# One decoder block on one core: the order of TensorE's instructions for the attention of tiles 4 to 7 is written out by hand

## The chip, the core and the metric

The kernel runs on one core of a Trainium2 chip. The time is the device time of one launch in microseconds (us); the median of three launches before the change is 1340.05 us (1338.88 to 1342.16). The engines go by their profile names: PE is TensorE (PEld its weight loads), DVE is VectorE, ACT is ScalarE, POOL is GpSimd, and SP is the queue that issues the DMAs.

## The reference, cut to what matters

The input x has 1024 tokens of 1024 columns, in float32. Cut to the parts that this case touches:

```
h = rmsnorm(x);  u_pool, q, kv, gates, B, C, X = split(h @ w_in)
y_nsa = gate0 * attend(q, k_cmp, v_cmp)            # 63 compressed keys
      + gate1 * attend(q, k of the 8 best blocks of 64)
      + gate2 * attend(q, k of the last 512 tokens)
x = x + concat(pool_mixer, y_nsa, short_conv) @ w_out
a, g = split(rmsnorm(x) @ ffn_up)                  # 2 x 2816 columns
x = x + (silu(causal_dwconv3(a)) * g) @ ffn_down
```

There are 8 heads of 64 in 2 groups g; a group shares its keys and values. The 8 best blocks come from the compressed scores.

## The kernel before, in words

**Tiles and products.** The 1024 tokens are 8 tiles of 128. Nearly every float32 product is done as three TensorE products, high times high, high times low part and low times high, where the high part is a rounded copy (ACT, line 88) and the low part the rest (DVE or POOL, line 89).

**One attention unit** is (i, g, br): tile i, group g and branch br, where br = 1 is the window (5 key tiles for i >= 4) and br = 0 the selected blocks (i + 1 key tiles). `span` gives the number ns. `scores` makes, for each of 4 heads, an S tile (two products per half, lines 570 and 571), adds the mask and takes the maximum (DVE, line 578), exponentiates into `pb` (ACT, line 581) and scales it (POOL, line 586). From tile 4 on there is one S tile (two PSUM banks), so a head's S waits until line 581 of the head before has read it. `values` takes, for each key tile, four transposes of `pb` into a `tr` bank (`flip`, line 97: the data is TensorE's stationary operand, loaded like weights, and the identity of 128 columns is streamed), splits the bank (`put_pt`, lines 476 and 477), and adds two products to the unit's `acc` bank (lines 607 and 608). `prepare` transposes the queries of a tile, `compressed` makes the compressed scores (lines 508 to 510), its probabilities `pc`, and the penalties `pen` of the blocks left out, which go into rows 96 to 111 of the query operand qB before the scores of br = 0.

**Order of the work.** `attend` walks over the units: it weaves the scores of a unit with the values of the unit before. It is called for tiles 0..3, then (line 805) for tiles 4..7. After this call in the program come: the projection of the pool and convolution parts of all tiles (`project`, lines 832 to 835), the projection of the attention part of tiles 0..3 with `second_norm` into `h2a`, the 22 chunks of `up` for tokens 0..511 (48 products of 512 columns each, lines 853 to 855, into two `fill` banks), 5 pairs of "early down" products into x2 (line 928, 48 products a pair, 6 per bank, added by DVE in line 929), and the projection of tiles 4..7 into x2. The last third of the time is the same for tokens 512..1023.

What an engine runs in which order is decided when the program is built, by a scheduler that goes by a model of the time and prefers what stands earlier in the program. So in the kernel before, attention of tiles 4..7 comes ahead of `up` and "early down" wherever it is ready, and these fill in. Each engine then runs its list in order: an instruction that waits holds up all behind it.

Of the kernel before, what the change touches and what calls it, by code (L numbers as in the profile page):

```python
# [1 line left out]

# [6 lines left out]
F32 = mybir.dt.float32  # L9
F32R = mybir.dt.float32r  # L10
# [18 lines left out]
NEG = -(2.0 ** 100)  # L29
FORCE = 1e6  # L30
QBUF = 1


C_POOL = 0
# [11 lines left out]
def kernel(  # L46
# [430 lines left out]
        dve.tensor_tensor(lo, pt, hi.bitcast(F32), ALU.subtract)  # L477
        return hi, lo

    qAs, pcs, yfs, pos = {}, {}, {}, {}  # L480
    new_s, new_p, m_row = [None], [None], [None]

    def prepare(i):

        qn = at2.tile([P, 512], F32, tag="qn", bufs=1, name=nm("qn"))
        nc.sync.dma_start(qn, qd[i])
        for g in range(2):
            pq = tr()
            for pr in range(2):
                c0 = g * 256 + pr * P  # L490
                flip(pq[:, pr * P : (pr + 1) * P], qn[:, c0 : c0 + P])
# [10 lines left out]
    def compressed(i):  # L502

        sc = tr()
        sc3 = sc.rearrange("p (h n) -> p h n", h=8)
        for h in range(8):
            g, hh = divmod(h, 4)
            pe.matmul(sc3[:, 2 * hh + g, :], qAs[i, g][:, hh, :], kca[g], start=h == 0, stop=False)
            pe.matmul(sc3[:, 2 * hh + g, :], qB[g][i % QBUF][0:66, hh, :], kcb[g][0:66, :], start=False, stop=False)
        pe.matmul(sc3, ident_b, m_cmp[:, i, :].unsqueeze(1).to_broadcast([P, 8, 64]), start=False, stop=True)  # L510
        mx = small(8, "mx8")
        dve.tensor_reduce(mx, sc3, axis=AX.X, op=ALU.max)
# [11 lines left out]
        if i >= 4:  # L524

            pen = at2.tile([P, 2, 16], F32, tag="pen", bufs=1, name=nm("pen"))
            for g in range(2):
                pg = small(64, "pg", bufs=2)
                dve.tensor_reduce(pg, pc[:, g::2, :].rearrange("p h n -> p n h"), axis=AX.X, op=ALU.add)
                p4 = pg.rearrange("p (j k) -> p j k", k=4)  # L530
                imp = small(16, "imp")
                dve.tensor_reduce(imp, p4[:, :, 0:3], axis=AX.X, op=ALU.add)
                dve.scalar_tensor_tensor(imp, p4[:, :, 3], 0.5, imp, ALU.mult, ALU.add)
                dve.scalar_tensor_tensor(imp[:, 1:16], p4[:, 0:15, 3], 0.5, imp[:, 1:16], ALU.mult, ALU.add)
                dve.tensor_tensor(imp, imp, sel_keep[:, i - 4, :], ALU.mult)
# [6 lines left out]
                pp = tr()  # L542
                flip(pp[0:16, 0:P], pen[:, g, :])
                act.activation(qB[g][i % QBUF][96:112, :, :], pp[0:16, 0:P].unsqueeze(1).to_broadcast([16, 4, P]), AF.Copy)


        pc4 = pc.rearrange("p (h g) n -> p g h n", g=2)
        for g in range(2):
# [1 line left out]
                               gat[:, i, 4 * g : 4 * g + 4].unsqueeze(2).to_broadcast([P, 4, 64]), ALU.mult)  # L550
        pt = tr()
        for hh in range(4):
            flip(pt[:, hh * P : (hh + 1) * P], pc[:, 2 * hh : 2 * hh + 2, :].rearrange("p g n -> p (g n)"))
        pcs[i] = put_pt(pt, "c")

    def span(i, br):
        s0 = max(0, i - 4) if br == 1 else 0
        return s0, i + 1 - s0

    def scores(i, g, br, pbs):  # L560
# [5 lines left out]
        for hh in range(4):  # L566
            S = new_s[0]()
            for c in range(nck):
                cols = slice(s0 * P + c * cw, s0 * P + (c + 1) * cw)
                pe.matmul(S[:, c, :cw], qAs[i, g][:, hh, :], kA[br, g][:, cols], start=True, stop=False)  # L570
                pe.matmul(S[:, c, :cw], qB[g][i % QBUF][0:krows, hh, :], kB[br, g][0:krows, cols],  # L571
                          start=False, stop=True)

# [15 lines left out]
            yield  # L589

    def values(i, g, br, pbs):

# [16 lines left out]
            yield  # L609
        if br == 1:  # L610
            return

        if g == 0:
            yfs[i] = at2.tile([P, 4, P], F32, tag="yf", bufs=1, name=nm("yf"))
        yb = at2.tile([P, 4, P], F32, tag="pth", name=nm("yb"))[0:64]
# [4 lines left out]
        if g == 1:  # L620
            if i < NT - 1:
                nc.sync.dma_start(yn[i], yfs[i])

    def weave(a, b, na, nb):

        done_b = 0
        for k in range(na):
            next(a, None)
            while done_b < (k + 1) * nb // na:
                next(b, None)  # L630
                done_b += 1
        for _ in a:
            pass
        for _ in b:
            pass

    def attend(tiles):
        prepare(tiles[0])
        compressed(tiles[0])
        prev = None  # L640
        for u in [(i, g, br) for i in tiles for g in range(2) for br in (1, 0)] + [None]:
            pbs = []
            sg = scores(*u, pbs) if u else iter(())
            vg, nv = iter(()), 0
            if prev:
                vg = values(*prev[0], prev[1])
                nv = span(prev[0][0], prev[0][2])[1] + (prev[0][2] == 1)
            weave(sg, vg, 3, nv)
            if u and u[1:] == (1, 0) and u[0] < tiles[-1]:
                prepare(u[0] + 1)  # L650
                compressed(u[0] + 1)
            prev = (u, pbs)


    f1 = pht.enter_context(tc.tile_pool(name="f1", bufs=7, side="right"))
# [146 lines left out]
    sth = ExitStack()  # L802
    h2p = sth.enter_context(tc.tile_pool(name="h2a", bufs=1, side="right"))
    h2a = [h2p.tile([P, KT, 512], F32R, name=n) for n in ("h2a_hi", "h2a_lo")]
    attend([4, 5, 6, 7])


    def load_wout(rows_, lo_engs):
# [8 lines left out]
            ws.append((wh, wl))  # L817
        return ws

    def project(y, ws, src, lo_eng, xr=None):  # L820

        if xr is None:
            xr = f4()
# [4 lines left out]
        for nh in range(2):  # L828
            wh, wl = ws[nh]
            ps = fill()  # L830
            for k in range(4):
                pe.matmul(ps, yh[:, k, :], wh[:, k, :], start=k == 0, stop=False)
                pe.matmul(ps, yh[:, k, :], wl[:, k, :], start=False, stop=False)
            for k in range(4):
                pe.matmul(ps, yl[:, k, :], wh[:, k, :], start=False, stop=k == 3)
            ns = slice(nh * 512, nh * 512 + 512)
            dve.tensor_tensor(xr[:, ns], ps, xr[:, ns], ALU.add)
        return xr

    def load_y(src):  # L840
# [1 line left out]
        nc.sync.dma_start(y, src)  # L842
        return y

    def up(c, hv, h2, gbank):

        wh, wl = load_w2(up_r, c * P, DFF + c * P, (pool, pool))
        pss = []
        for sub in range(2):
            ps = (gbank if sub else fill)()  # L850
            cols = slice(sub * P, (sub + 1) * P)
            for kt in range(KT):
                pe.matmul(ps, wh[:, kt, cols], h2[0][:, kt, :], start=kt == 0, stop=False)  # L853
                pe.matmul(ps, wh[:, kt, cols], h2[1][:, kt, :], start=False, stop=False)  # L854
                pe.matmul(ps, wl[:, kt, cols], h2[0][:, kt, :], start=False, stop=kt == KT - 1)  # L855
            pss.append(ps)
        a, g = pss
# [44 lines left out]
    for c in range(NCH):  # L902
        v = up(c, 0, h2a, fill)
        nc.sync.dma_start(hid0[c], v)
    sth.close()


    xp = ctx.enter_context(tc.tile_pool(name="x2", bufs=1, side="right"))
    x2 = xp.tile([P, NT, D], F32, name="x2")


    for i in range(4):
        nc.sync.dma_start(x2[:, i, :], xb[i])
    for c0 in range(0, EARLY, 2):
        dhl = [w([P, 2, D]) for w in (whi, wlo)]
        hhl = []
        for k in range(2):
            hhl.append([f2.tile([P, 512], F32R, tag=t, bufs=2, name=nm(t)) for t in ("yh", "yl")])
            hidden_in(c0 + k, *hhl[k], pool)
            down_in(c0 + k, dhl[0][:, k], dhl[1][:, k], pool)  # L920
        for i in range(4):
            tt = slice(i * P, (i + 1) * P)
            for nh in range(2):
                ns = slice(nh * 512, nh * 512 + 512)
                ps = fill()
                for k in range(2):
                    for a, b in ((0, 0), (0, 1), (1, 0)):
                        pe.matmul(ps, hhl[k][a][:, tt], dhl[b][:, k, ns], start=k + a + b == 0, stop=k + a == 2)  # L928
                dve.tensor_tensor(x2[:, i, ns], ps, x2[:, i, ns], ALU.add)


    ws = load_wout((2, 4), (pool, dve))
    for i in range(4, NT):
        project(load_y(yn[i]) if i < NT - 1 else yfs[i], ws, xa[i], dve, x2[:, i, :])


    st3.close()
# [90 lines left out]
```

## Time and profile before

| | |
|---|---|
| median of 3 launches | 1340.05 us |
| profiled execution | 1340.74 us; from its first to its last instruction (the span) 1339.0 us |
| busy share of the span | PE 97%, PEld 81%, DVE 57%, ACT 40%, POOL 38% |
| mean granted TensorE clock | 0.992 of the full 2.4 GHz |
| first `up` product, last "early down" product | 440.45 us, 874.62 us |

All stretches are in us from the span's start. Matmuls overlap in the records, since each row shows a product from its start to its result: what a product costs PE is read from the distance of its start to the next start, and not from its length.

### The profile page before, as it was taken

The numbers are of one execution on the slowest core, as the hardware profiler recorded it, in microseconds if no ns is written. First come the engines' busy times: TensorE is split into PE (matmuls) and PEld (weight loads), VectorE is DVE, ScalarE is ACT, GpSimd is POOL, SyncE is SP. The second block draws the span as 40 slices with busy tenths as digits, with TensorE's granted clock in tenths as the row PEclk, the third lists the DMA queues.
The fourth block names the chain that finished last, engine by engine and source line by source line (L and its number), as shares of the span: only waits on it lengthen the run. The fifth ranks groups of instructions, "written<-read, shape, count | busy, mean of one in ns | idle before, by whom it ended". The sixth has DMA issues, their size and how long they took to land.

```text
span 1339.0 us, 17613 instructions
## 1 busy us (share of the span) xinstructions
PE 1298.8 (97%) x6510; PEld 1081.2 (81%) x6510; DVE 764.2 (57%) x1487; ACT 541.9 (40%) x978; POOL 504.0 (38%) x452
## 2 busy tenths in 40 slices
PE   6999999989988999999999999999999999999998
PEld 5899987678866888888888888777888788888886
DVE  6753456666666545545645667675454545455554
ACT  5442444344465554445444464443232213223330
POOL 3454722341343445344444544533333124222220
PEclk9999999989998999999999999999999999999999
DMA  9021220335432323322222272323242225323321
GB/s 263 14 64 52 81 84 16 97 126 179 154 108 78 110 87 112 94 78 88 79 89 77 93 264 85 95 81 93 63 126 67 76 78 158 93 81 104 99 64 64
DMA packets 143075, 131.02 MB, mean 98 GB/s; under 512 B 10659, under 2 KB 119437, under 8 KB 142989
## 3 DMA queue, kind: packets, MB, share of 16 engines
q1 hardware_dynamic: 142845, 129.80, 31.3%
q8 instruction: 51, 0.84, 0.2%
q14 instruction: 35, 0.29, 0.1%
q10 hardware_dynamic: 144, 0.10, 0.0%
HBM read 107.60 MB, written 22.28 MB: 97 GB/s over the span
## 4 chain that ended last, share of the span: by engine, by line
PE 89%; DVE 4%; DMA 3%; ACT 2%; issue 1%; POOL 0%; SPq 0%; ACTq 0%; DVEq 0%; POOLq 0%
PE dn L972 12%; PE fill L853 9%; PE fill L855 9%; PE fill L854 9%; PE tr L97 4%; PE fill L928 4%; PE upg L853 3%; PE upg L855 3%; PE upg L854 3%; PE S L570 2%; PE fill L211 2%; PE S L571 2%; PE fill L212 2%; PE fill L213 2%; PE acc L608 2%; PE acc L607 2%
## 5 line engine op out<-in xcount | busy, mean ns | idle before, releaser
L89 POOL TENSOR_TENSOR wlo<-wst,whi 128x1024 fp32r<-128x1024 f32 x113 | 273.5, 2434 | 305.4 <-ACT whi L88 305.2
L586 POOL TENSOR_SCALAR pb<-pb,rc,gat 128x640 f32<-128x640 f32 (+7 forms) x128 | 105.4, 825 | 294.1 <-DVE rc L584 276.8
L88 ACT ACTIVATE whi<-wst 128x1024 fp32r<-128x1024 f32 x128 | 131.1, 1055 | 136.0 <-DMA wst<-in_ffn_up_dram 80.7
L853 PE MATMUL fill<-h2a_hi,whi 128*128 128x512 f32 x352 | 141.1, 401 | 0.1
L854 PE MATMUL fill<-h2a_lo,whi 128*128 128x512 f32 x352 | 140.8, 400 | 0.0
L855 PE MATMUL fill<-h2a_hi,wlo 128*128 128x512 f32 x352 | 140.8, 400 | 0.0
L581 ACT ACTIVATE pb<-S,mx 128x640 f32<-128x640 f32 (+7 forms) x128 | 89.3, 699 | 105.8 <-DVE mx L578 96.4
L975 DVE TENSOR_TENSOR x<-dn,x 128x1024 f32<-128x1024 f32 x64 | 78.2, 1221 | 89.0 <-PE dn L972 88.8
L477 DVE TENSOR_TENSOR ptl<-tr,pth 128x512 fp32r<-128x512 f32 x140 | 93.9, 686 | 52.7 <-ACT pth L476 26.1
L476 ACT ACTIVATE pth<-tr 128x512 fp32r<-128x512 f32 x140 | 80.5, 596 | 76.2 <-PE acc L607 38.4
L860 DVE SCALAR_TENSOR_TENSOR f2k<-fill,colw,f2k 128x511 f32<-128x511 f32 x44 | 32.9, 748 | 87.7 <-ACT f2k L859 83.8
L97 PE MATMUL tr<-ident,pb 128*128 128x128 f32 x528 | 82.8, 272 | 0.1
L578 DVE CUSTOM_DVE_ANT_0 S<-S,m_win 128x640 f32<-128x640 f32 (+4 forms) x96 | 57.7, 607 | 41.4 <-PE S L571 40.9
L972 PE MATMUL dn<-dh,hh 128*128 128x512 f32 x256 | 79.1, 391 | 0.5 <-DVE x L975 0.5
L972 PE MATMUL dn<-dh,hl 128*128 128x512 f32 x256 | 79.2, 391 | 0.0
L972 PE MATMUL dn<-dl,hh 128*128 128x512 f32 x256 | 79.0, 390 | 0.0
L570 PE MATMUL S<-blk,qA 128*128 128x320 f32 (+5 forms) x192 | 67.0, 352 | 11.2 <-ACT pb L581 11.2
L97 PEld LDWEIGHTS tr<-ident,pb 128*128 128x128 f32 x528 | 66.0, 140 | 14.5 <-POOL pb L586 0.3
L853 PEld LDWEIGHTS fill<-h2a_hi,whi 128*128 128x128 f32 x352 | 66.3, 188 | 14.0 <-DVE h2a_lo L181 0.4
L855 PEld LDWEIGHTS fill<-h2a_hi,wlo 128*128 128x128 f32 x352 | 66.3, 188 | 13.7
L854 PEld LDWEIGHTS fill<-h2a_lo,whi 128*128 128x128 f32 x352 | 66.3, 188 | 13.5
L853 PE MATMUL upg<-h2b_hi,whi 128*128 128x512 f32 x176 | 69.1, 393 | 1.0 <-ACT whi L88 0.9
(275 smaller groups left out, 3175.8 us busy)
## 6 DMA issues: line engine op xcount, KB each, us to landing
wst<-in_ffn_up_dram SPq DMA_DIRECT2D x88, 512.0 KB, 3.9
wst<-in_ffn_down_dram SPq DMA_DIRECT2D x32, 512.0 KB, 3.6
wst<-in_w_in_dram SPq DMA_DIRECT2D x18, 512.0 KB, 4.1
wst<-in_w_out_dram SPq DMA_DIRECT2D x12, 512.0 KB, 4.3
hid<-f2k SPq DMA_DIRECT2D x22, 256.0 KB, 2.0
f2k<-hid SPq DMA_DIRECT2D x22, 256.0 KB, 2.9
b<-in_x_dram SPq DMA_DIRECT2D x8, 512.0 KB, 7.0
f<-in_x_dram SPq DMA_DIRECT2D x8, 512.0 KB, 4.2
```

The lines of the kernel that those rows point to most:

```text
L88: act.activation(hi, src, AF.Copy)
L89: lo_eng.tensor_tensor(lo, src, hi.bitcast(F32), ALU.subtract)
L97: pe.transpose(out, src, ident[:n, :n])
L476: act.activation(hi, pt, AF.Copy)
L477: dve.tensor_tensor(lo, pt, hi.bitcast(F32), ALU.subtract)
L570: pe.matmul(S[:, c, :cw], qAs[i, g][:, hh, :], kA[br, g][:, cols], start=True, stop=False)
L581: act.activation(pb[:, : ns * P].rearrange("p (c n) -> p c n", c=nck), S, AF.Exp, bias=mx, scale=-1.0, accum_out=sw)
L586: pool.tensor_scalar(pb[:, : ns * P], pb[:, : ns * P], rc, gat[:, i, col : col + 1], ALU.mult, ALU.mult)
L853: pe.matmul(ps, wh[:, kt, cols], h2[0][:, kt, :], start=kt == 0, stop=False)
L854: pe.matmul(ps, wh[:, kt, cols], h2[1][:, kt, :], start=False, stop=False)
L855: pe.matmul(ps, wl[:, kt, cols], h2[0][:, kt, :], start=False, stop=kt == KT - 1)
L972: pe.matmul(ps[:, nh - turn[0], :], h[:, tt], w[:, nh * 512 : nh * 512 + 512], start=k == 0 and h is hh and w is dh, stop=k == n - 1 and h ...
```

## The change

`values` is replaced, for tiles 4..7, by `value_steps`, and `prepare` and `compressed` become generators that stop before each PE instruction with its kind ("t" for a transpose or a 64-column product, "p" for another product) and a place x in its slot. `slots` has one slot per unit: the unit's scores (its heads at 0.02, 0.22, 0.42 and 0.62 of the slot), the values of the unit before (0.08 to 0.95), and, in the slots of the units (i, 1, 0) of tiles 4 to 6, the next tile's queries (0.75), compressed scores (0.92) and, reaching into the next slot, the transposes of pc (1.7) and pen (1.85). The slot of unit (4, 0, 1) (`LEAD` = 1) stands where `attend` stood. The others are merged with `fillers`, that is `up` and then "early down", under a `manual_schedule` for PE alone: PE's instructions of this region run in the order in which they are written, the other engines stay with the scheduler, and so does the place of PE instructions from outside of the region among these. In `merge`, 380 us are shared out among the slots by key tiles; a filler is counted as 0.231 us, a transpose as 0.03 us, any other step as 0.2 us, fillers are laid until the next step's place is reached, and one is put between two "t" steps.

```diff
+STEP = 0.231
+LEAD = 1
+ATT_US = 380.0
...
+    def value_steps(i, g, br, pbs, x0, x1):
+        s0, ns = span(i, br)
+        n = 6 * ns + 4
...
+        for s in range(ns):
+            if br == 1 and s == 1:
+                pos[i, g] = ps2.tile([P, 512], F32, tag="acc", name=nm("acc"))
+                queue[i, g][0:0] = [((i, g), vvc[:, g, :], w, w is pcs[i][0], False) for w in pcs[i]]
+            pt = tr()
+            for hh in range(4):
+                yield "t", x0 + (x1 - x0) * k / n
+                k += 1
+                flip(pt[:, hh * P : (hh + 1) * P], pbs[hh][:, s * P : (s + 1) * P])
+                if hh in (1, 3) and queue[i, g] and not (br == 1 and s == 0):
+                    yield "p", x0 + (x1 - x0) * k / n
+                    k += 1
+                    product()
+            parts = put_pt(pt)
...
+    def merge(slots, us, filler):
...
+                while at < e[0] and fill_one():
+                    at += STEP
+                    short = False
+                at = max(at, e[0])
+                if e[2] == "t" and short and fill_one():
+                    at += STEP
+                if e[2] != "head":
+                    short = e[2] == "t"
+                    at += 0.03 if short else 0.2
...
-    attend([4, 5, 6, 7])
+    second = list(slots([4, 5, 6, 7]))
+    for _, streams in second[:LEAD]:
+        for st in streams:
+            run(st)
...
+        for c0 in range(0, EARLY, 2):
...
+                hhl.append([f2.tile([P, 512], F32R, tag=t, bufs=2, name=nm(t)) if c0 % 4 == 0 else f2k(F32R) for t in ("yh", "yl")])
...
+    filler = fillers()
+    with tc.manual_schedule(engines={pe.engine}):
+        merge(second[LEAD:], ATT_US, filler)
+    run(filler)
```

Two smaller edits are in it: every second pair of "early down" takes its four operand tiles from the five `f2k` buffers in place of `yh` and `yl` (two buffers each), and `compressed` transposes pen after pc in place of before.

## Rows read from the trace of the kernel before

**Rows 1.** Stretch, length, busy us of PE, PEld, DVE, ACT, POOL, clock, DMA.

```profile
285.00:440.40 155.40, 142.25 (x705) 114.92 (x703) 106.25 (x253) 80.36 (x174) 56.54 (x59) 0.95 0.43 143
440.40:874.90 434.50, 433.89 (x2148) 359.91 (x2148) 250.18 (x521) 210.68 (x360) 198.62 (x129) 1.00 0.32 101
```

**Rows 2.** PEld's longest wait in 440.4 to 874.9: total, times, longest.

```profile
PEld fill L928 <- DVE x L929: 0.8, 1, 0.8
```

**Rows 3.** PE in order of time (start, length), a lone transpose between products.

```profile
446.26 0.40 PE L608 MATMUL acc<-ptl,vv 128*128 128x512 f32 x1
446.50 0.27 PE L97 MATMUL tr<-ident,pb 128*128 128x128 f32 x1
446.52 0.48 PE L855 MATMUL fill<-h2a_hi,wlo 128*128 128x512 f32 x1
446.85 0.39 PE L853 MATMUL fill<-h2a_hi,whi 128*128 128x512 f32 x1
```

**Rows 4.** PE in order of time, three transposes in a row between products.

```profile
448.23 0.49 PE L97 MATMUL tr<-ident,pb 128*128 128x128 f32 x3
...
448.80 0.39 PE L854 MATMUL fill<-h2a_lo,whi 128*128 128x512 f32 x1
```

**Rows 5.** PEld in order of time, the weight loads of the two products behind the lone transpose.

```profile
446.50 0.19 PEld L855 LDWEIGHTS fill<-h2a_hi,wlo 128*128 128x128 f32 x1
446.61 0.19 PEld L853 LDWEIGHTS fill<-h2a_hi,whi 128*128 128x128 f32 x1
```

**Rows 6.** Groups of PE's instructions in 431.8 to 440.4 (count | busy, mean ns).

```profile
L97 PE MATMUL tr<-ident,pb 128*128 128x128 f32 x20 | 2.8, 272 | 0.0
L608 PE MATMUL acc<-ptl,vv 128*128 128x512 f32 x4 | 2.0, 493 | 0.0
L607 PE MATMUL acc<-pth,vv 128*128 128x512 f32 x4 | 1.7, 434 | 0.0
L570 PE MATMUL S<-blk,qA 128*128 128x320 f32 x4 | 1.4, 353 | 0.0
L571 PE MATMUL S<-blk,qB 112*128 112x320 f32 x4 | 1.2, 318 | 0.0
...
L598 PE MATMUL acc<-ptl,vvc 128*128 128x512 f32 x1 | 0.5, 496 | 0.6 <-DVE ptl L477 0.6
...
L597 PE MATMUL acc<-pth,vvc 128*128 128x512 f32 x1 | 0.5, 474 | 0.0
```

**Rows 7.** The chain of waits that ended last, 432.5 to 440.5 us.

```profile
432.53 0.70 DVE f L837
...
436.86 0.61 DVE ptl L477
...
437.90 0.59 ACT pth L476
...
439.12 0.68 DVE ptl L477
...
440.45 0.50 PE fill L853
```

**Rows 8.** Two stretches of rows 1's kind, before and after PE starts again at 294.96.

```profile
289.00:294.90 5.90, 2.29 (x11) 1.50 (x9) 5.28 (x14) 3.71 (x7) 5.53 (x5) 0.92 0.55 150
294.90:300.90 6.00, 5.94 (x14) 4.68 (x15) 3.17 (x4) 1.20 (x4) 4.82 (x5) 0.51 1.05 410
```

**Rows 9.** PE in order of time, the second and third head's first S product [idle before].

```profile
416.64 0.46 PE L570 MATMUL S<-blk,qA 128*128 128x320 f32 x1 [2.18 <-ACT pb L581]
...
419.81 0.63 PE L570 MATMUL S<-blk,qA 128*128 128x320 f32 x1 [1.90 <-ACT pb L581]
...
423.73 0.64 PE L570 MATMUL S<-blk,qA 128*128 128x320 f32 x1 [0.61 <-ACT pb L581]
```

**Rows 10.** Start of "early down": SP's load of x2, and DVE's first additions.

```profile
779.07 0.80 SPq L913 DMA_DIRECT2D x<-xb  x2
...
784.37 1.29 DVE L929 TENSOR_TENSOR x<-fill,x 128x512 f32<-128x512 f32 x2
```

More of the change, by code (lines that the diff above doesn't have):

```diff
@@ L1 @@
 from contextlib import ExitStack
+from itertools import chain
 import concourse.bass as bass
@@ L478, in put_pt, with run, queries @@
         return hi, lo
-    qAs, pcs, yfs, pos = {}, {}, {}, {}
+    qAs, pcs, yfs, pos, queue = {}, {}, {}, {}, {}
     new_s, new_p, m_row = [None], [None], [None]
-    def prepare(i):
+    def run(steps):
+        for _ in steps:
+            pass
+    def queries(i, x=0.0):
         qn = at2.tile([P, 512], F32, tag="qn", bufs=1, name=nm("qn"))
@@ L588, in scores @@
             pbs.append(pb)
-            yield
+            yield "head", x
     def values(i, g, br, pbs):
@@ L611, in values, with finish @@
             return
+        finish(i, g)
+    def finish(i, g):
+        po = pos[i, g]
         if g == 0:
@@ L627, in weave @@
         for k in range(na):
-            next(a, None)
+            for kind, _ in a:
+                if kind == "head":
+                    break
             while done_b < (k + 1) * nb // na:
@@ L637, in attend @@
     def attend(tiles):
-        prepare(tiles[0])
-        compressed(tiles[0])
+        run(queries(tiles[0]))
+        run(compressed(tiles[0]))
         prev = None
@@ L649, in attend, with slots @@
             if u and u[1:] == (1, 0) and u[0] < tiles[-1]:
-                prepare(u[0] + 1)
-                compressed(u[0] + 1)
+                run(queries(u[0] + 1))
+                run(compressed(u[0] + 1))
             prev = (u, pbs)
+    def slots(tiles):
+        units = [(i, g, br) for i in tiles for g in range(2) for br in (1, 0)]
+        pbs = {}
+        for k in range(len(units) + 1):
+            streams, size = [], 0
+            if k < len(units):
+                u = units[k]
+                pbs[k] = []
+                size += span(u[0], u[2])[1]
+                if k == 0:
+                    streams += [queries(u[0]), compressed(u[0])]
+                streams.append(scores(*u, pbs[k], 0.02, 0.2))
+            if k > 0:
+                v = units[k - 1]
+                size += span(v[0], v[2])[1]
+                streams.append(value_steps(*v, pbs.pop(k - 1), 0.08, 0.95))
+            if k < len(units) and u[1:] == (1, 0) and u[0] < tiles[-1]:
+                streams.append(chain(queries(u[0] + 1, 0.75), compressed(u[0] + 1, 0.92, 1.7, 1.85)))
+            yield size, streams
@@ new lines, in merge, with fill_one @@
+    def merge(slots, us, filler):
+        total = sum(size for size, _ in slots)
+        at = 0.0
+        short = False
+        live = []
+        def fill_one():
+            return next(filler, None) is not None
+        begin = 0.0
+        for size, streams in slots:
+            length = us * size / total
+            for st in streams:
+                step = next(st, None)
+                if step:
+                    live.append([begin + step[1] * length, len(live), step[0], st, begin, length])
+            begin += length
+            while live:
+                live.sort(key=lambda e: e[0])
+                e = live[0]
+                if e[0] >= begin:
+                    break
+                while at < e[0] and fill_one():
+                    at += STEP
+                    short = False
+                at = max(at, e[0])
[4 more added lines that the diff above has]
+                    at += 0.03 if short else 0.2
+                step = next(e[3], None)
+                if step is None:
+                    live.pop(0)
+                else:
+                    e[0], e[2] = max(e[0], e[4] + step[1] * e[5]), step[0]
+        for e in sorted(live, key=lambda e: e[0]):
+            run(e[3])
@@ L837, in project @@
             dve.tensor_tensor(xr[:, ns], ps, xr[:, ns], ALU.add)
+    def project(y, ws, src, lo_eng):
+        xr = f4()
+        run(project_steps(y, ws, src, lo_eng, xr))
         return xr
@@ L843, in load_y, with up, up_steps @@
         return y
-    def up(c, hv, h2, gbank):
+    def up(*args):
+        steps = up_steps(*args)
+        while True:
+            try:
+                next(steps)
+            except StopIteration as e:
+                return e.value
+    def up_steps(c, hv, h2, gbank):
         wh, wl = load_w2(up_r, c * P, DFF + c * P, (pool, pool))
@@ L901 @@
         second_norm(i, xr, h2a)
[L902 to L920, printed above, removed]
-        for i in range(4):
[L922 to L929, printed above, removed]
+    x2_ = []
```

72 lines of the change are left out of this document (63 added, 9 removed).

## The prediction

> **What bounds the kernel now.** I read the stretches first, to see where PE has room: from the first `up` product to the last "early down" product PE is busy for 433.9 of 434.5 us at a full clock, while DVE, ACT and POOL are busy for half of it or less [rows 1]. The stretch before it, 285 to 440.4, has PE idle for 13 us and a clock of 0.95. Then I read PEld's waits in the full stretch: the longest is one of 0.8 us [rows 2]. So where the change works there is nearly no stall that a better order could take away; what it can win there is only PE time itself, by making an instruction cheaper. For that I read PE in order of time around single transposes [rows 3 to 5], and for what it can lose, the last 8 us before the first `up` product [rows 6, 7].
>
> **What a transpose costs, alone and in a row.** From the start of the lone transpose (446.50) to the start of the second product behind it (446.85) are 0.35 us [rows 3]. A product of 512 columns costs 0.234 us (446.26 to 446.50), so the transpose costs 0.116. It is easily misread: the next product's record starts 0.02 us behind the transpose, but that record is 0.48 us long in place of 0.40, and the one behind it starts 0.33 later. Three in a row, from 448.23 to the second product behind (448.80), are 0.57 us; less 0.234 that is 0.112 each [rows 4]. The weight loads say why: the load for the product behind the transpose starts with it, at 446.50, the load after that at 446.61, 0.11 us later [rows 5]; the transpose's own short stream cannot hide it. With a neighbour of either kind the price is 0.11 us, so "no two transposes in a row" saves nothing. For the 398 transposes of the region (92 key tiles times 4, and 12 each for queries and pc and 6 for pen of tiles 5 to 7), I take 0 us. As the other bound, at the 0.03 us that `merge` counts (the 0.02 between two records, taken for a price), they would be 398 x (0.11 - 0.03) = 32 us cheaper; rows 3 exclude it, since they show just the pattern that the change lays.
>
> The Trainium skill, page "TensorE: Matmul & The Clock Gate", has a rule for each side. Its section "Step-by-step: what each phase is for" says that the engine pulls weight loads ahead of running matmuls; read alone, it leaves a transpose between products little more than its own 128 columns, 55.6 ns by the page's formula, and would make the sum 398 x 0.055 = 22 us lower. Its section "LDWEIGHTS (loading the stationary operand)" gives 107 ns for 128 columns, which a 128-column stream cannot cover in either order, and leaves the sum as it is; by that rule, the trace agrees (0.11 between two loads).
>
> **What is moved: the start.** In the kernel before, attention fills the wait for `h2a`: between the last projection of tile 3 and the first `up` product PE runs 20 transposes of pb, 8 S products and 10 products into acc [rows 6]: 20 x 0.11 + 8 x 0.146 + 10 x 0.234 = 5.7 us (an estimate by columns for an S product: 320 of 512, of 0.234 us). All of it belongs to the slots that are now in the region. Followed by hand, `merge` lays one `up` product first: two fillers are asked for before the first head's place at 0.02 of a 21 us slot, and the first request stops short of its product. That product needs all of `h2a`, and PE keeps the written order, so none of the 5.7 us can run before `h2a` is there. What comes back: the chain from line 837 to line 853 takes 7.9 us and has on it two ptl pieces of 0.61 and 0.68 and a pth of 0.59 of just this attention [rows 7]; without them `h2a` is ready at most 1.9 us earlier. I take 1.8. **Cost 5.7 - 1.8 = 3.9 us**; between 3.3 (the chain ahead of it also gains 0.5 by the S products that stood in line 835's way) and 5.7.
>
> With PE idle for some 6 us there, but for 8 transposes of the norm, the clock is a second matter. Around 292 PE worked 2.3 of 5.9 us, and when it began again it ran 6 us at 0.51, the lower level (1.2 GHz): 14 products in 6.0 us where 0.234 each makes 3.3 [rows 8]. **Cost 2.7 us**, taken whole since the idle time is as long; bounds 0 (no drop) and 5.
>
> **Inside of the region.** I counted the distances in the laid order with these prices. The high-part product of a key tile comes 2.4 to 15.9 us behind its last transpose (middle 5.4), a unit's first transpose 12 us or more behind its last scores: no wait. Per slot the four heads stand over 4 us apart, with one exception: behind the compressed scores, the first two heads of unit (5, 0, 1) are 2.5 us apart, those of (6, 0, 1) 3.3 (in between stands nothing but their own S and a few fillers). There is one S tile; its turn took 3.2 and 3.9 us at half clock [rows 9], less 0.5 for the four S products, which take some 0.6 us at full clock and twice that at half, 2.7 and 3.4. That is 0.2 to 0.9 us late, more where the compressed maximum comes in between on DVE: **1.0 us**, bounds 0.2 and 2.9. The `acc` bank is needed again 6 us after its last product, and what reads it is one copy and two additions, none longer than a pth piece of 0.6 [rows 7]: free. The DMAs of the moved steps (three query loads, three yn stores, all on SP) have a slot of time on either side, and POOL's scalings and splits stay with the scheduler, on an engine that is busy for 198.6 of 434.5 us [rows 1]: free.
>
> At the change to "early down" x2 takes the place of `h2a`, so its load can only be issued behind the last `up` product. Before, from the issue (779.07) to the end of the first addition (half of 784.37 + 1.29) were 6.0 us [rows 10], and the scheduler had put attention into it. The laid order has 4.1 us between the first down product and the third bank, which needs that addition; with the issue 0.3 after the start: 0.3 + 6.0 - 4.1 = **2.2 us**; bounds 0 (a quicker load) and 4 (other loads ahead on SP). What is late next is covered: each further tile of x2 is asked for 3 us later. The f2k edit lets a pair's operands be prepared during the pair before, and is costed at nothing: in the last pairs there are 12 us for it.
>
> **The end.** The attention is done some 22 us before the region's last product, which covers the tile 7 wait; the project stage behind it is unchanged: 0.
>
> **Sum**: 0 + 3.9 + 2.7 + 1.0 + 2.2 = 9.8 us. The profiled execution took 1340.74 us, so 1350.5; it stands 0.7 above the median, hence **1349.9 us**. The bounds add up to 3.5 and 17.6 us, or 1343.6 to 1357.7.
>
> **The rivals.** (1) Faster: the transpose's price falls between products, as `merge` counts. Then 32 us come off and the other terms stay: 1340.0 + 9.8 - 32 = 1318. It decides if a lone transpose costs under 0.085 (9.8 us over 398). Against it stand rows 3 and the same price of one and three in a row; for it, only the 0.02 us between two starts. Chance 0.08; with some gain in the scheduler's part before 440 (13 us are idle there), faster altogether 0.11. The rule of the Trainium skill on loads pulled ahead (same page, "Step-by-step: what each phase is for") would put this rival at 1328, and shares its chance. (2) No change that can be told: what this kernel's measurement can tell is about 0.3%, 4 us. The clock does not drop, x2 lands in time and the chain shortens fully: 3.3 to 4 us, 1343.5. For it speaks that the other engines have half their time free [rows 1]. Chance 0.24. (3) Slower still: "early down" is starved. Every second pair holds four of the five f2k buffers, so the next pair's two hidden chunks pass one after the other through the last one: a load, a split on ACT and on POOL. If that takes 16 us (a load as slow as x2's [rows 10] and two splits for each chunk) against the 12 us of the last laid pairs, PE stands still for 4 us at two pairs: 1349.9 + 8 = 1358. It decides where a pass takes over 6 us; SP's crowded stretch speaks for it, half-idle POOL against. Chance 0.12. That the change does not do what it says can hardly be: the region's order is the written one; only the transposes outside (the first slot's, the norms') may still stand in a row.
>
> **How the numbers follow.** Forecast 0.53 at 1349.9, rivals 0.11, 0.24 and 0.12. The range leaves out rival 1, the better half of rival 2 and the far end of rival 3: 1339 to 1360. Faster 0.11; same 0.24 and a little of the forecast, 0.25; slower 0.64.
>
> **What would show it.** Right: lone transposes still 0.11 us, no two in a row behind the first `up` product, PE idle for about 6 us just before it, some microseconds of half clock there, one wait for line 929's first addition, and the stretch to the last down product 441 us and more where it was 434.5. Wrong: a start-to-start price of a lone transpose near 0.03 (then rival 1), or no idle time before the first `up` product.

## The result, and the profile after

| | before | after |
|---|---|---|
| median | 1340.88 us (6 runs) | 1349.80 us (6 runs, 1348.22 to 1351.46) |
| after : before | | 1.0067, interval 1.0054 to 1.0080 |
| profiled execution, its span | 1340.74, 1339.0 us | 1350.91, 1349.2 us |
| mean granted clock | 0.992 | 0.988 |
| first `up` product | 440.45 us | 438.92 us |
| last "early down" product | 874.62 us | 883.28 us |
| from the one to the other | 434.17 us | 444.36 us |

The kernel became slower by 8.9 us in the median and by 10.2 us between the two profiled executions. The forecast was 1349.9 us. The lines of the changed kernel have other numbers: transposes are on line 104, S products on 590 and 592, acc products on 659, `up` on 996, 998 and 1000, "early down" products on 1076 and their additions on 1077, the load of x2 on 1060, the split of a weight on 95 (ACT) and 96 (POOL or DVE), the norm on 178, 187 and 188.

The stretches of the changed kernel, with the columns of [rows 1]:

```profile
431.70:438.90 7.20, 2.33 (x10) 1.57 (x8) 2.97 (x5) 3.21 (x6) 4.45 (x4) 0.67 0.69 218
438.90:444.30 5.40, 5.38 (x16) 4.29 (x17) 1.65 (x4) 2.43 (x4) 3.77 (x3) 0.50 0.35 99
438.90:883.30 444.40, 442.52 (x2185) 355.72 (x2185) 249.34 (x529) 211.59 (x365) 200.28 (x129) 0.99 0.31 99
```

In the 7.2 us ahead of the first `up` product PE is busy for 2.3; the granted clock, which fell at 434.1 in this wait, stands at half for the first 5.4 us of the region. The region has 2185 PE instructions, 37 more than [rows 1] had, which is the moved work within one record (20 transposes, 8 S products and 10 products into acc). PE in order of time shows the wait itself, on the norm of tile 3 (start, length, idle before):

```profile
436.36 1.97 PE L104 MATMUL fill<-ident,f 128*128 128x128 f32 x8 [4.30 <-DVE f L178]
438.92 0.79 PE L996 MATMUL fill<-h2a_hi,whi 128*128 128x512 f32 x1 [0.59 <-DVE h2a_lo L188]
439.51 0.47 PE L590 MATMUL S<-blk,qA 128*128 128x320 f32 x1
```

The waits of PE's weight loads from there to the last "early down" product, to be held against [rows 2], which had one of 0.8 us:

```profile
PEld fill L1076 <- DVE x L1077: 2.6, 2, 1.6
PEld fill L996 <- DVE h2a_lo L188: 1.0, 1, 1.0
PEld S L590 <- ACT pb L602: 0.5, 1, 0.5
```

A transpose in the laid order, PE by time, in the pattern of [rows 3]:

```profile
444.50 0.39 PE L996 MATMUL fill<-h2a_hi,whi 128*128 128x512 f32 x1
444.74 0.27 PE L104 MATMUL tr<-ident,pb 128*128 128x128 f32 x1
444.76 0.47 PE L998 MATMUL fill<-h2a_lo,whi 128*128 128x512 f32 x1
445.08 0.39 PE L1000 MATMUL fill<-h2a_hi,wlo 128*128 128x512 f32 x1
```

From 444.74 to the second product behind it, at 445.08, are 0.34 us, of which a product takes 0.23: 0.11 for the transpose, as before. In the chain that ended last, the steps just ahead of the first `up` product stand in the place of [rows 7]:

```profile
432.20 4.31 DMA wst<-in_ffn_up_dram
...
436.60 1.06 ACT whi L95
437.66 0.49 ACT h2a_hi L187
...
438.17 0.70 DVE h2a_lo L188
...
438.92 0.79 PE fill L996
```

The pieces of ptl and pth have left the chain. In their place a weight's load and its split on ACT stand ahead of h2a_hi. An emptier DVE alone would hardly bring the start forward: in the run with spare transposes in the wait, further down, the norm's own transposes take 1.09 us in place of 1.97, and the same split, from 437.15 to 438.21, still stands ahead of h2a_hi in the chain.

The two waits on line 1077 have two causes. At the first, SP issues the load of x2 at 809.37, and DVE's first addition has waited 1.23 us for it:

```profile
809.37 0.80 SPq L1060 DMA_DIRECT2D x<-xb  x2
813.29 0.69 DVE L1077 TENSOR_TENSOR x<-fill,x 128x512 f32<-128x512 f32 x1 [1.23 <-DMA x<-xb]
```

In the kernel before, the first addition [rows 10] did not wait for its load. The load landed 4.1 us behind its issue (3.8 in the changed kernel), at 783.16, and DVE then was still taking a head's maximum:

```profile
782.98 1.23 DVE L578 CUSTOM_DVE_ANT_0 S<-S,m_row 128x1024 f32<-128x1024 f32 x1 [0.28 <-PE S L571]
```

At the second, 60 us later, DVE itself is late. It has the split of an output weight (line 96) in its queue ahead of an addition. DVE and then PE by time:

```profile
873.24 2.52 DVE L96 TENSOR_TENSOR wlo<-wst,whi 128x1024 fp32r<-128x1024 f32 x1
875.68 1.27 DVE L1077 TENSOR_TENSOR x<-fill,x 128x512 f32<-128x512 f32 x2
```

```profile
876.41 0.50 PE L1076 MATMUL fill<-whi,yh 128*128 128x512 f32 x1 [1.17 <-DVE x L1077]
```

### The profile page after: what moved, and what is told of

Read it like the earlier page. It is cut to its first block, busy times and chain, and to the rows that moved or that the text cites. A ratio compares the mean times of both kernels' runs of the same rounds, so it can differ in the third digit from the quotient of the medians.

```text
span 1349.2 us, 17653 instructions
## 1 busy us (share of the span) xinstructions
PE 1302.3 (97%) x6510; PEld 1073.0 (80%) x6510; DVE 760.2 (56%) x1487; ACT 539.8 (40%) x978; POOL 504.0 (37%) x452
## 4 chain that ended last, share of the span: by engine, by line
PE 86%; DVE 5%; DMA 4%; issue 2%; ACT 2%; POOL 1%; SPq 0%; ACTq 0%; POOLq 0%; DVEq 0%
PE dn L1126 12%; PE fill L996 9%; PE fill L1000 9%; PE fill L998 9%; PE tr L104 4%; PE acc L659 3%; PE fill L1076 3%; PE upg L996 3%; PE upg L1000 3%; PE upg L998 3%; PE fill L218 2%; PE fill L219 2%; PE S L590 2%; PE fill L220 2%; PE S L592 2%
## 5 line engine op out<-in xcount | busy, mean ns | idle before, releaser
L996 PE MATMUL fill<-h2a_hi,whi 128*128 128x512 f32 x352 | 150.1, 426 | 0.6 <-DVE h2a_lo L188 0.6
L1000 PE MATMUL fill<-h2a_hi,wlo 128*128 128x512 f32 x352 | 150.0, 426 | 0.0
L998 PE MATMUL fill<-h2a_lo,whi 128*128 128x512 f32 x352 | 149.8, 426 | 0.0
L104 PE MATMUL tr<-ident,pb 128*128 128x128 f32 x528 | 126.9, 273 | 0.1
L104 PEld LDWEIGHTS tr<-ident,pb 128*128 128x128 f32 x528 | 72.0, 141 | 16.9 <-POOL pb L607 0.3
```

The source lines that it names most:

```text
L104: pe.transpose(out, src, ident[:n, :n])
```

## The experiments

The theory: a transpose costs 0.11 us wherever it stands, so the laid order wins nothing, and it loses what the kernel before did while it waited for `h2a`, with a clock drop behind that wait and a few waits of the fixed order. The rivals: a lone transpose is cheaper and something else hides the gain; or early down starves on f2k. Every edit is made to the changed kernel unless the text says otherwise. "Region" is the time from the first `up` to the last "early down" product of the profiled run.

**Transposes in a row again.** The four transposes of a key tile follow each other with no filler between; the two products keep their places behind.

```diff
-                yield "t", x0 + (x1 - x0) * k / n
+                yield "t", x0 + (x1 - x0) * k0 / n
...
-                if e[2] == "t" and short and fill_one():
-                    at += STEP
```

> The changed kernel, with the four transposes of a key tile laid in a row again and no filler put between them; where attention stands among the fillers stays as it is. Theory (a transpose costs 0.11 us alone and in a row): within 3 us of the changed kernel, 1347 to 1353 us, with transposes 0.11 us apart. Rival 1 (a lone transpose costs 0.03 us and the loss came from elsewhere): 368 x 0.08 = 29 us slower, about 1379.

Measured: 1350.46 us, 1.0076 of before (1.0063 to 1.0089); region 444.04. PE by time, one row of four:

```profile
446.63 0.40 PE L1000 MATMUL fill<-h2a_hi,wlo 128*128 128x512 f32 x1
446.86 0.60 PE L104 MATMUL tr<-ident,pb 128*128 128x128 f32 x4
447.22 0.48 PE L996 MATMUL fill<-h2a_hi,whi 128*128 128x512 f32 x1
447.54 0.40 PE L998 MATMUL fill<-h2a_lo,whi 128*128 128x512 f32 x1
```

From 446.86 to 447.54 are 0.68 us; less 0.234 that is 0.45 for four, 0.11 each. Undoing the spreading neither gains nor loses: the filler between two transposes is worth nothing.

**Every transpose twice, alone and in a row.** Each of the 368 transposes of pb is made twice into the same place, once with a filler between the two, once with eight in a row. The work added is the same; only the neighbours differ.

```diff
                 flip(pt[:, hh * P : (hh + 1) * P], pbs[hh][:, s * P : (s + 1) * P])
+                yield "t", x0 + (x1 - x0) * (k - 0.5) / n
+                flip(pt[:, hh * P : (hh + 1) * P], pbs[hh][:, s * P : (s + 1) * P])
```

Alone:

> The changed kernel, with each of the 368 transposes of pb done twice into the same place, with a filler between the two. Theory: 368 x 0.11 = 40 us more, 1390 us (1386 to 1396). Rival 1: 368 x 0.03 = 11 us more, 1361.

Measured: 1390.40 us, 1.0374 (1.0358 to 1.0390); the 40.6 us over the changed kernel are 0.110 for each of 368.

In a row (the same line added to the first experiment's kernel, where the second stands at the first one's place):

> The kernel with four transposes in a row, each of the 368 done twice: eight in a row. Theory: 368 x 0.11 = 40 us over the kernel with four in a row, 1390 us, and within 3 us of the one with lone doubled transposes. Rival 1 agrees on the 40 us here, but has the lone ones 29 us below.

Measured: 1393.32 us, 1.0398 (1.0384 to 1.0412), 42.9 over the first experiment. Of these, 1.9 are a longer wait on an x2 addition (2.2 us of PE's time in place of 0.3) and 1.7 a clock drop behind it (half of 3.4 us); the rest, 39.3, is 0.107 for each of 368. PE by time with eight in a row:

```profile
445.87 1.04 PE L104 MATMUL tr<-ident,pb 128*128 128x128 f32 x8
446.66 0.48 PE L998 MATMUL fill<-h2a_hi,whi 128*128 128x512 f32 x1
446.97 0.39 PE L1000 MATMUL fill<-h2a_lo,whi 128*128 128x512 f32 x1
```

From 445.87 to 446.97 are 1.10 us; less 0.234 that is 0.108 each. PE by time with the lone ones:

```profile
447.87 0.27 PE L104 MATMUL tr<-ident,pb 128*128 128x128 f32 x1
447.90 0.48 PE L998 MATMUL fill<-h2a_hi,whi 128*128 128x512 f32 x1
448.21 0.27 PE L104 MATMUL tr<-ident,pb 128*128 128x128 f32 x1
```

From transpose to transpose are 0.34 us, with one product of 0.23 between. The 0.03 us from a transpose's start to the next start is no price: the product behind it pays, with 0.31 to the start after its own. The price is 0.11 with either neighbour, and the first rival falls.

**No fixed order.** The steps are handed to the scheduler as before, without the order written out for TensorE.

```diff
-    with tc.manual_schedule(engines={pe.engine}):
-        merge(second[LEAD:], ATT_US, filler)
+    merge(second[LEAD:], ATT_US, filler)
```

> The changed kernel without the manual_schedule: the same steps in the same order in the program, but PE's order is the scheduler's. Theory (the loss is the start, where the written order holds attention behind the first up product): PE has attention in the 7 us before the first up product, no drop of the clock at 434, and 5 to 8 us come off: 1342 to 1345 us. Rival (the loss is due to the stretch behind it, the even spread or the f2k edit): idle time of 5 us ahead of the first up product is filled, but the time stays within 2 us of 1350.

Measured: 1342.21 us (10 runs), 1.0015 (1.0006 to 1.0024). The stretches, columns as above:

```profile
431.70:442.90 11.20, 8.77 (x53) 6.68 (x51) 7.34 (x15) 8.29 (x16) 8.29 (x6) 1.00 0.60 187
442.90:875.70 432.80, 432.73 (x2141) 356.97 (x2141) 245.89 (x519) 208.39 (x355) 195.46 (x127) 1.00 0.32 100
```

PE is busy again while it waits for `h2a` (8.8 of 11.2 us), the clock stays full, and PE is busy for 432.7 of the region's 432.8 us. So some 7 of the 9 us are in the fixed order, and not in the other edits. About 2 us remain, by an interval that leaves out 1: in the profile the region is 1.4 us shorter than before, but it begins 2.5 us later, since a weight split behind a load of 5.5 us and the exponential of a head stand ahead of h2a_hi on ACT.

**Idle time without moved work.** 28 spare transposes of xr, which nothing reads, stand in the wait for `h2a`; the moved work stays behind it. This measures the clock's share alone.

```diff
         nc.sync.dma_start(xb[i], xr)
+        if i == 3:
+            spare = new_s[0]()
+            for _ in range(28):
+                flip(spare[:, 0, 0:P], xr[:, 7 * P : 8 * P])
         second_norm(i, xr, h2a)
```

> The changed kernel with 28 spare transposes of tile 3's projected rows into the S tile, which nothing reads, placed in the wait between the projection and the norm's transposes. Nothing of the attention moves. Theory of the clock (an idle PE of 4.5 us brings the lower level, which then lasts into the up products): the drop at 434 goes, the way from the first up product to the last down product shrinks from 444.4 to about 441.7 us, 1347 us (1346 to 1348.5). Rival (the lower level costs nothing here): 1350 us.

Measured: 1347.07 us, 1.0046 (1.0033 to 1.0059): 2.7 us under the changed kernel's median, region 442.04, 2.3 shorter. The stretches:

```profile
431.70:439.40 7.70, 5.16 (x40) 4.23 (x38) 3.41 (x6) 4.15 (x7) 4.88 (x4) 1.00 0.66 204
439.40:444.90 5.50, 5.42 (x29) 4.46 (x30) 2.37 (x6) 2.54 (x4) 4.50 (x3) 1.00 0.35 103
```

With PE busy for 5.2 of 7.7 us the drop is gone, and a region that does the same work is shorter by about what half of 5.4 us at half clock makes. It begins 0.6 us later, at 439.48.

**Moved work put back, first try.** Two slots in place of one are left to the scheduler ahead of the laid order, so more attention can stand in the wait.

```diff
-LEAD = 1
+LEAD = 2
-ATT_US = 380.0
+ATT_US = 359.0
```

> The changed kernel with two slots ahead of the region in place of one (LEAD = 2; the 380 us cut to 359, so that attention stands as dense among the fillers as before). Theory: the 20 transposes, 8 S products and 10 acc products may again run in the wait for h2a, PE has no idle time of 4 us there and no half clock: 5.7 + 2.7 - 1.5 = 7 us off, 1343 us (1341 to 1346). Rival (the written order behind the first up product costs the time): within 2 us of 1350.

Measured: 1354.49 us, 1.0100 (1.0085 to 1.0116), a miss by 11 us. PE by time shows why:

```profile
438.81 0.49 PE L996 MATMUL fill<-h2a_hi,whi 128*128 128x512 f32 x1 [0.69 <-DVE h2a_lo L188]
440.96 0.41 PE L590 MATMUL S<-blk,qA 128*128 128x320 f32 x1 [1.66 <-ACT pb L602]
...
443.89 0.64 PE L590 MATMUL S<-blk,qA 128*128 128x320 f32 x1 [2.07 <-ACT pb L602]
...
447.23 0.64 PE L590 MATMUL S<-blk,qA 128*128 128x320 f32 x1 [1.90 <-ACT pb L602]
```

Three heads' scores stand in a row behind the first `up` product, and each waits until ACT has read the one S tile for the head before. PE is idle for 5.6 us here, the clock stands at half from 443.0 to 453.2, and the region takes 449.2 us. A second drop, of 3.4 us at 825, stands behind a wait of 1.8 us on an x2 addition.

**Moved work put back, second try.** The first 12 us of the laid places get no fillers, so that the attention steps there come first.

```diff
-        at = 0.0
+        at = first = 12.0
...
-                if e[2] == "t" and short and fill_one():
+                if e[2] == "t" and short and e[0] >= first and fill_one():
```

> The changed kernel, with no filler laid among the attention steps of the region's first 12 us of places: about 13 transposes, 12 S products and 6 acc products stand ahead of the first up product, PE still in the written order. Theory: these 4.6 us run in the wait for h2a, and the clock holds: 4.6 + 2.7 - 1.5 = 6 us off, 1344 us (1342 to 1347). Rival (it is the pinning itself that costs, not what stands first): within 2 us of 1350.

Measured: 1348.95 us, 1.0059 (1.0045 to 1.0073). The region is 5.4 us shorter (438.97). By the prediction's prices 5.6 us of work are out of it (17 transposes, 16 S products and 6 acc products), and the half clock at its start lasts 3.4 us in place of 5.4; a new wait for the S tile at 722 takes some 0.6 us of this back, and the rest of the difference was not traced. But it begins at 442.38. PE by time:

```profile
433.73 0.41 PE L590 MATMUL S<-blk,qA 128*128 128x320 f32 x1 [2.02 <-ACT pb L602]
...
437.33 0.42 PE L590 MATMUL S<-blk,qA 128*128 128x320 f32 x1 [0.62 <-ACT pb L602]
...
441.66 0.41 PE L590 MATMUL S<-blk,qA 128*128 128x320 f32 x1 [2.21 <-ACT pb L602]
...
442.38 0.65 PE L996 MATMUL fill<-h2a_hi,whi 128*128 128x512 f32 x1
```

The same turns of the S tile now hold up the first `up` product: the fourth head starts only at 441.66.

**Moved work put back, third try.** Only the value steps of unit (4, 0, 1) are laid ahead; the S heads keep their places.

```diff
     with tc.manual_schedule(engines={pe.engine}):
+        run(second[LEAD][1].pop())
         merge(second[LEAD:], ATT_US, filler)
```

> From the changed kernel, the value steps of unit (4,0,1) (20 transposes, at most 10 products with acc, some 4.3 us of TensorE by 20 x 0.11 + 9 x 0.234) stand ahead of the first up product; the four S heads of unit (4,0,0) stay behind it, spread as they were. Theory (the changed kernel loses its time because TensorE has nothing to do in the wait for h2a, so that the work done there before now stands behind it, and the clock drops; the two trials that put S heads into or next to the wait missed because heads in a row wait for the one S tile): no drop of the clock at 434, first up product back at about 440.4 because the copies are again on VectorE beside the norm (+1.5), first up to last down shorter by 4.3 + 2.7 = 7.0; in all 1350 - 5.5 = 1344.5 us (1343 to 1346.5). Rival (any work of the attention placed in the wait comes out even, as in the trials with the S heads: it waits for its own inputs, pb from POOL here, and delays the norm by as much): 1348.5 to 1351.

Measured: 1352.46 us (4 runs), 1.0083 (1.0063 to 1.0103); the profiled one took 1347.73 and the others 1352.45 to 1353.62. The spread was larger than the effect, so the same kernel ran again:

> The same kernel as e10_values_ahead, in five rounds, because its four runs lay 5 us apart (1347.73 for the profiled one, then 1352.45 to 1353.62), more than the gain that was asked for. If the profiled run of e10 is what the edit gives, these runs lie at 1346 to 1349 with the same stretches. If the others are, they lie at 1351 to 1354, and the profile, when it is of such a run, shows where: by the theory that the place of work in the wait decides the clock, a drop of 10 us in place of 3.4 (3.4 us of it lost); by the rival that early down products and upg wait for other engines in turns that differ from run to run, waits longer by 4 us in all between 800 and 1100, with the clock as in e10.

Measured: 1352.41 us (6 runs, 1346.93 to 1353.79), 1.0078 (1.0059 to 1.0097), the profiled one 1351.96. The value steps do stand in the wait in both. Yet the region takes 442.45 us in the first profile and 444.73 in the second, in place of the 437.4 expected. PE's waits in the region, first and second profile:

```profile
PE S L590 <- ACT pb L602: 1.1, 1, 1.1
PE tr L104 <- DVE ptl L484: 0.8, 1, 0.8
```

```profile
PE S L590 <- ACT pb L602: 1.1, 1, 1.1
PE tr L104 <- DVE ptl L484: 2.3, 3, 1.1
```

The clock was expected to hold, but in both profiles it stands at half for 3.4 us behind the wait, so 1.7 of the 5.0 us missing in the first are the clock's. And with 4 us of work out of the region, later steps come before their operands: a wait of 1.1 us for pb, where the changed kernel has one of 0.2, and waits for ptl that it has not on PE. In the second profile two of these stand around 531 us, not behind 800 where longer waits were looked for, behind this on DVE, with this on POOL:

```profile
525.63 4.30 DVE L556 TENSOR_SCALAR pen<-rp 128x16 f32<-128x16 f32 x2
```

```profile
525.15 4.75 POOL L96 TENSOR_TENSOR wlo<-wst,whi 128x1024 fp32r<-128x1024 f32 x2
```

Two DVE instructions of 16 columns take 4.30 us, for as long as POOL splits two weights. The changed kernel has the same pair in 0.23 us, at 528.06, 1.25 us before POOL's splits begin. That is 1.9 us of PE time (waits of 0.59 and 1.32), most of the 2.3 between the two regions. Another 2.6 us between these two profiles lie before the first `up` product, and 2.5 of them before the wait, in code that the edit does not touch: the last projection product of tile 3 starts at 429.75 and 432.25. A part is there from the start on: products of 268 columns start 0.22 us apart up to 15.3 us in the first profile and up to 17.4 in the second, and 0.12 apart behind that. The rest was not traced.

**The last 2 us of the wait filled too.** The kernel of the third try with 18 of the spare transposes.

> e10_values_ahead with 18 spare transposes of xr, which nothing reads, in the wait for h2a (2.0 us of TensorE beside the 4.3 of the value steps). Theory: the clock has no drop at 438.8, where e10 lost half of 3.4 us, so 1.7 us less than e10 in the same call; first up product not over 0.5 us later. Rival (the drop costs nothing that is not lost anyway to waits behind it): the same as e10 within 1 us, although the drop is gone.

Measured: 1352.25 us (6 runs), 1.0081 (1.0066 to 1.0095): no faster than the third try. The clock holds behind the wait:

```profile
441.00:444.50 3.50, 3.42 (x16) 2.92 (x17) 1.14 (x3) 2.03 (x3) 1.63 (x2) 1.00 0.52 151
```

but the region takes 444.65 us, since a wait for ptl behind the product at 630.5 is now 3.3 us long (1.0 in the third try), again behind a pair of pen instructions of 4.25 us beside two splits on POOL.

**The kernel before, with its S waits filled.** Spare products and transposes stand between the S heads of unit (4, 0, 1) in the kernel before, where the clock had dropped around 417.

```diff
             weave(sg, vg, 3, nv)
+            if u == (4, 0, 1):
+                spare = ps2.tile([P, 512], F32, tag="acc", name=nm("acc"))
+                for _ in range(10):
+                    pe.matmul(spare, qAs[4, 0][:, 0, :], kA[0, 0][:, 0:512], start=True, stop=True)
+                for _ in range(14):
+                    flip(spare[:, 0:P], pbs[0][:, 0:P])
```

> The kernel before, with 10 spare products of 512 columns and 14 spare transposes, which nothing reads, in the two waits for the S tile of unit (4, 0, 1) around 415 and 419 us. Theory of the clock: the drop at 417 goes (10.2 us at the lower level, in which PE is busy for 7.7), 3.8 us off, 1336.5 us. Rival: the clock falls anyway, or the spare work holds up the scores behind it: 1340 to 1343 us.

Measured: 1342.95 us (11 runs) against 1341.53, 1.0014 (1.0005 to 1.0022), a miss. The drop shrank from 10.2 to 3.4 us, but the start of the region did not move, since ACT decides it, and a new drop of 3.4 us stands behind that start, from 441.8 to 445.2 (clock 0.50); the region is 1.3 us longer. ACT by time, before and then with the spare work:

```profile
438.85 0.60 ACT L180 ACTIVATE h2a_hi<-fill 128x512 fp32r<-128x512 f32 x1
440.04 1.06 ACT L88 ACTIVATE whi<-wst 128x1024 fp32r<-128x1024 f32 x1 [0.59 <-DMA wst<-in_ffn_up_dram]
```

```profile
438.33 1.06 ACT L88 ACTIVATE whi<-wst 128x1024 fp32r<-128x1024 f32 x1 [1.50 <-DMA wst<-in_ffn_up_dram]
439.30 1.07 ACT L180 ACTIVATE h2a_hi<-fill 128x512 fp32r<-128x512 f32 x2
```

The order of the two has turned: h2a_hi now stands behind a weight split that waits 1.5 us for its DMA. The first `up` product starts at 440.65, where it was 440.45, though this run is 2.4 us ahead of the other by 290 us and its last projection product of tile 3 starts 3.3 us earlier (428.84 against 432.10).

**Early down on one set of operand buffers.** All pairs take yh and yl, none f2k.

```diff
-                hhl.append([f2.tile([P, 512], F32R, tag=t, bufs=2, name=nm(t)) if c0 % 4 == 0 else f2k(F32R) for t in ("yh", "yl")])
+                hhl.append([f2.tile([P, 512], F32R, tag=t, bufs=2, name=nm(t)) for t in ("yh", "yl")])
```

> From the changed kernel, all five pairs of early down products take yh and yl for their operands, as the kernel before does, none takes f2k. Theory (the second set of operand buffers costs nothing and is needed now that pairs follow each other within 11 to 18 us): each of four changes of pair waits for the operands of the next, which can be loaded and split only when the last product of the pair before is done: 1 to 4 us each, 1354 to 1366 us. Third rival of the prediction (the f2k buffers starve the early down products of what else lives in them): without them 1346 us or less. Between (1348.5 to 1351.5): the buffers of the operands make no difference in either direction, and the two waits of early down products in the changed kernel (0.88 and 1.33 us) have to do with the x2 adds alone.

Measured: 1357.06 us, 1.0126 (1.0109 to 1.0143), 7.3 us over the changed kernel. PE's waits:

```profile
PE fill L1076 <- DVE x L1077: 3.8, 3, 3.1
PE fill L1076 <- POOL yl L96: 2.8, 5, 1.4
```

A wait for POOL's yl appears at the changes of pair, which the changed kernel has nowhere, and the waits on x2 additions grow by 2.0 us. The f2k edit pays for itself, and the third rival falls.

## Why the prediction was right, point by point

**Transposes, 0 us: right.** 0.110 us is the median of 274 lone ones that stand between products of 512 columns in the changed kernel, and 0.110 that of 76 rows of four in the first experiment. Spreading them (first experiment) and doubling them (two more) both show it. The Trainium skill, page "TensorE: Matmul & The Clock Gate", section "LDWEIGHTS (loading the stationary operand)", gives P / 1.2 ns for the load of P columns, by which 107 ns is an estimate for 128; the runs agree, with 0.11. The rule of its section "Step-by-step: what each phase is for" on loads pulled ahead, read alone with the 55.6 ns that it gives for 128 columns, would have given a lone transpose half of that, by this estimate; no run here shows such a price.

**The start, 3.9 us: right in size, 4.2 by the runs.** The moved 5.7 us are out of the wait and in the region: PE is busy for 2.3 of its 7.2 us, most of it the norm's own transposes, and the region has the 37 more instructions. PE was idle for 4.9 us there, where some 6 had been said. The first `up` product came 1.5 us earlier where 1.8 was taken; 1.1 of this is a shorter wait and 0.4 an earlier last projection product (431.67 against 432.10). The reason given was only half of it: DVE's and ACT's pieces for attention did leave the chain, but a weight's DMA and split are what is left on it. Two readings are off without moving the sum: the first `up` product does not need all of `h2a`, since the second half of tile 3's h2a_hi is made only at 440.77, behind it; and DVE is busy for 58% of the region (250.18 of 434.5 us [rows 1]), not for half or less.

**The clock, 2.7 us: right.** 5.4 us at half clock, and 2.7 us of the median (2.3 of the region) come back when the wait is filled with work that nothing needs.

**S heads, 1.0 us: less,** one wait of 0.5 us of the weight loads, 0.2 of it PE's own, at 515.5 in unit (5, 0, 1) as predicted, and none at (6, 0, 1). **The x2 wait, 2.2 us: mis-sized.** It was 0.9 us of PE's time: the first addition started 3.9 us behind the issue and ended 4.6 behind it, where 6.0 had been taken over from [rows 10]. Those 6.0 were not the load's alone: it had landed after 4.1, and then DVE's maximum of a head held the addition up for 1.2 us more. With 4.6 in place of 6.0 the prediction's own sum gives 0.8. Besides it there is a second wait of 1.3 us on the same line that the prediction did not see: DVE's split of an output weight, made 2.52 us long, ahead of an addition. "Covered" was said of each further tile of x2, and DVE's own queue was not asked.

**The sum.** 5.7 + 2.7 + 0.9 + 1.3 + 0.2 = 10.8, less the 0.8 us that the kernel before waited in its own region [rows 2], is 10.0; the region grew by 10.2. With the start 1.5 earlier that leaves 8.7. The rest of the 10.2 us, 1.5, lies behind the region (465.9 us against 464.4 between the profiles). Of that stretch the prediction had said 0; other kernels of the study with the same code there took 464.2 (eight in a row) to 466.1 (first experiment), so it may be the spread between runs; it was not traced further.

That the forecast came within 0.1 us of the median is luck: the three large steps (nothing won by spreading, the moved work, the clock) were right, but 2.1 us too much for the S heads and the x2 load were made up, in the main, by a second wait that was not seen and by the stretch behind the region.

**The rivals.** (1) fell with the doubled transposes. (2) asked for no drop, x2 in time and a chain shortened in full; the first two were shown false by the profile. (3) fell: f2k is what keeps early down fed.

**What was wrong are five expectations of the study,** all on the same step: that work put into the wait is won. It costs turns of the one S tile (first and second try), or runs ahead of its producers later on (third try, also with the last 2 us filled), or leaves the start on ACT's weight split (kernel before with its S waits filled). No version tried beats the kernel before; of the changed kernel's the nearest is the scheduler's own order, 1.0015.

## What to carry to other kernels

Price an instruction by the distance to the second start behind it, and test the price by doubling it in place: the gap behind a short one is paid by its neighbour. An order written out for one engine removes the scheduler's freedom to fill a wait, so look first at what the old order did in each wait, since that work, and the clock drop behind an idle engine, are the bill. Putting it back by hand needs an order in which every step's producers, buffers and queues on the other engines are in time too; freeing PE time in front only helps as far as those keep up.

## What was not expected of the hardware

A DVE instruction that reads and writes 16 columns took 2.2 us on average (4.30 for two) when it fell beside POOL's weight split, and 0.12 (0.23 for two) when it did not. In the changed kernel the DVE split at 873.24 took 2.52 us while POOL's own split (2.40 us from 872.28) was running. In the kernel before, where DVE's split started first, at 860.40, it took 1.26, and POOL's, from 860.54, took 3.39. Between the two profiles of the third try this was worth 1.9 us of PE's time, and so is part of why ten runs of one kernel lay 6.9 us apart; eight of the ten were not profiled. The Trainium skill, page "SBUF — State Buffer", section "Who interferes with whom", says that the two engines share a pair of ports, and that where both want it the instruction that issues first holds it until it ends. The two pairs of pen agree: 4.30 beside 4.75 us of POOL, 4.25 beside 4.70. In the first profile of the third try only one of two pen instructions was held, 2.01 us for the pair beside 4.75 of POOL.
